# Decoder trunk on one core: where the second sums, a down half's last weights and the first seven-product chunk's weights are cast

## The chip, the cores and the metric

The kernel runs on one core of one Trainium2 chip. The metric is the device time of one launch in microseconds, as the median of several runs. One core has five engines with a queue each: PE (TensorE, matmuls; the profile shows its weight loads apart, as PEld), ACT (ScalarE), DVE (VectorE), POOL (GpSimd) and SP (SyncE, which here only issues loads of weights).

## What is computed

A decoder trunk of two layers on 512 tokens with 1024 features, all in float32. Each layer has a half-step SwiGLU network, a mixer, and a second half-step SwiGLU network; the first mixer is gated linear attention, the second a stick-breaking attention.

```python
D_MODEL = 1024
SEQ = 512
DEPTH = 2
D_FF = 2816

def swiglu(h, w_gate, w_up, w_down):
    return (jax.nn.silu(h @ w_gate) * (h @ w_up)) @ w_down

    for i in range(DEPTH):
        x = x + 0.5 * swiglu(rmsnorm(x, ffn1_norm[i]), ffn1_w_gate[i], ffn1_w_up[i], ffn1_w_down[i])
        h = rmsnorm(x, mix_norm[i])
        j = i // N_MIXERS
        if i % N_MIXERS == 0:
            y = gla_mixer(h, gla_w_in[j], gla_w_gk2[j], gla_b_gk[j], gla_o_norm[j], gla_w_out[j])
        else:
            y = sb_mixer(h, sb_w_in[j], sb_w_out[j])
        x = x + y.astype(x.dtype)
        x = x + 0.5 * swiglu(rmsnorm(x, ffn2_norm[i]), ffn2_w_gate[i], ffn2_w_up[i], ffn2_w_down[i])
    return rmsnorm(x, final_norm)
```

The change touches only the four SwiGLU networks, called FFN1 to FFN4 here (FFN1 and FFN2 lie around the first mixer, FFN3 and FFN4 around the second).

## The kernel before

**Split products.** Every float32 operand is cut into a high part, cast on ACT, and a low part, operand minus high part, made on DVE. A product is three matmuls: high times high, low times high, high times low. For weights the cast is L138 (names wh<-raw, wh<-rawd, wh<-s) and the low part L139 (wl); for activations both stand in `cut` (L838 and L839: nh/nl, th/tl, hh/hl).

**Stages.** FFN1 runs to about 337 us of the span, FFN2 from 545 to 870, FFN3 from there to 1206, FFN4 from 1414 to the end. Each has 11 chunks of 256 hidden columns, in groups (0,2), (2,4), (4,6), (6,8), (8,9), (9,11). For each chunk the gate product comes, then the up product. A group's down products follow later, between the chunks of the next groups.

**Seven products.** From chunk 2 on (`SEVEN`), gate and up are done as 2x2 blocks with seven products in place of eight (`seven`, L733 for the matmuls). Such a chunk has two entries in the list of work. `body_1` has three weights: a11 (128x512), the first sums s12 (128x1024) and a2 (128x1024). It makes product one into a PSUM bank w, has ACT copy w to z (L761, written ps_z<-ps_w), and goes on with product two into q, product three into w again and product four into z; L765 and L769 take q and w out in between. Product three may only write over w when the copy has read it. `body_2` has one weight, the second sums s34 (128x1024), for products five and six, and takes the other half of a2 for product seven. Sums are made on DVE (L718 and L719 for s12, L724 and L725 for s34).

The down products of groups 1 and 3 are done in the same way, in two halves each (`seven_down`, L394 for the matmuls). "First" to "fourth half" below are these in the order of an FFN. A half takes two loads of 128x1024, into two buffers named rawd. Its `body_1` has a11, the sums s12, and a2, which consists of two pieces of 128x512, one from each of the two loads; it makes two w products (for m of 0 and 1), copies both to z (L412), and has the products t1, t2 and b21, of which only b21 needs a2. Its `body_2` has the sums s34 for t3 and b22, ACT copies each w to a buffer u (L439, u<-ps_w) behind t3, and t4, with the other part of a2, writes over w. Results are added to x on DVE (L400).

**What sets the order.** `Feed.start` runs when an entry begins. It casts the weights of this entry and the two after it (`split`), as far as four buffers of 128x1024 suffice, makes the sums of one entry more, and issues the loads of six. Loads go out on SP, in order; a load waits until the last reader of its buffer is done. There are two buffers raw (1 MB) and two rawd (512 KB). A scheduler then puts the instructions of each engine into one order, from priorities, which `ahead` raises for what stands in it. `tc.issue_after(ins)` ties an instruction behind another. The chunks before `SEVEN` are plain blocks; `evac_u` (L886) makes the product of gate and up, and `close` cuts it to hh and hl for the down products, L80 ps_d.

The lines that the change starts from:

```python
            for e in self.q[i : i + 3]:
                used += sum(n * m >= 1024 for _, _, n, m in e.units)
                if used > 4:
                    break
                e.split()
            for e in self.q[i : i + 4]:
                e.view()
```

## Time and profile before

| what | value |
|---|---|
| median of 3 runs | 1778.77 us (1778.58 to 1780.93) |
| the profiled execution | 1778.36 us, span 1776.4 us |
| granted TensorE clock, mean | 0.999 |
| FFN1, FFN2, FFN3, FFN4 in the span | about 25 to 337, 545 to 870, 870 to 1206, 1414 to 1776 us |
| instructions | 31377 |

Rows of the profile are read thus: engine, line and operation, then what it writes and reads (`wl<-rawd,wh`), then shapes. In a timeline the first two numbers are start and duration in us; brackets tell how long the engine was idle before, and what released it. A row of the waits says who waited for whom, then total us, times, and the longest. Starts of neighbouring instructions on one engine lie closer together than their durations, since the next begins while the last drains; so a sequence is added up by starts.

### The profile page before, as it was taken

The page shows a single profiled execution, that of the slowest core. Times are in us where ns is not written, and L with a number is a line of the kernel's source. Part 1 is how long each engine was busy: PE and PEld are TensorE (multiplying, and loading weights), DVE is VectorE, ACT ScalarE, POOL GpSimd, SP SyncE. Part 2 cuts the span into 40 slices and gives each one's busy share as a digit, 9 for nine tenths or more (in the row PEclk, how much of TensorE's full clock was granted, in tenths as well). Part 3 has the DMA queues.
Part 4 walks back from the last instruction along what each step waited for, and adds up shares of the span by engine and source line. Part 5 has one row for each costly group of instructions (what it writes and reads, how often), then busy time and mean ns, then how long its engine had stood idle before and what let it go on. Part 6 is the DMA issues. An engine that isn't in the chain of part 4 may idle for free.

```text
span 1776.4 us, 31377 instructions
## 1 busy us (share of the span) xinstructions
PE 1755.4 (99%) x12714; PEld 1630.6 (92%) x12714; DVE 1509.6 (85%) x2474; ACT 1079.6 (61%) x1883; POOL 55.6 (3%) x77
## 2 busy tenths in 40 slices
PE   9999999999999999999999999999999999999998
PEld 8999999889888899999889999999888888999997
DVE  8999797786888989888798988967898679997986
ACT  7556556554655566555655555655888755565564
POOL 0000000200000000000000000010000000000000
PEclk9999999999999999999999999999999999999999
DMA  5543435422123433444434344342212234434441
GB/s 167 154 120 119 125 102 148 113 66 73 54 90 100 121 117 120 119 120 125 129 95 133 102 125 126 118 120 83 84 48 72 72 95 131 126 104 123 120 138 52
DMA packets 186388, 193.14 MB, mean 109 GB/s; under 512 B 4930, under 2 KB 171124, under 8 KB 186244
## 3 DMA queue, kind: packets, MB, share of 16 engines
q1 hardware_dynamic: 177760, 175.91, 31.7%
q0 software_dynamic: 8240, 14.95, 4.6%
q8 instruction: 99, 1.62, 0.4%
q14 instruction: 45, 0.37, 0.1%
q10 hardware_dynamic: 244, 0.29, 0.0%
HBM read 175.17 MB, written 2.10 MB: 100 GB/s over the span
## 4 chain that ended last, share of the span: by engine, by line
PE 60%; DVE 30%; ACT 5%; issue 3%; DMA 2%; SPq 0%; DVEq 0%; ACTq 0%
PE ps_w L733 13%; PE ps_d L80 12%; DVE wl L139 9%; PE ps_f L80 7%; PE ps_q L733 6%; PE ps_t L80 4%; PE ps_z L733 3%; PE ps_b L80 3%; PE ps_w L394 3%; ACT wh L138 2%; DVE x L400 2%; DVE hl L839 1%; PE ps_q L394 1%; DVE ts L848 1%; PE ps_z L1424 1%
## 5 line engine op out<-in xcount | busy, mean ns | idle before, releaser
L139 DVE TENSOR_TENSOR wl<-raw,wh 128x1024 fp32r<-128x1024 f32 x241 | 255.5, 1061 | 59.4 <-ACT wh L138 58.8
L138 ACT CAST wh<-raw 128x1024 fp32r<-128x1024 f32 x241 | 221.6, 920 | 77.8 <-PE ps_f L80 22.6
L139 DVE TENSOR_TENSOR wl<-s,wh 128x1024 fp32r<-128x1024 f32 x176 | 214.6, 1219 | 50.7 <-ACT wh L138 50.7
L733 PE MATMUL ps_w<-th,wh 128*128 128x256 f32 x864 | 239.4, 277 | 6.3 <-ACT ps_z L761 6.3
L733 PE MATMUL ps_w<-th,wl 128*128 128x256 f32 x864 | 237.6, 275 | 0.0
L733 PE MATMUL ps_w<-tl,wh 128*128 128x256 f32 x864 | 237.6, 275 | 0.0
L138 ACT CAST wh<-s 128x1024 fp32r<-128x1024 f32 x176 | 184.1, 1046 | 69.6 <-DVE s L719 19.4
L733 PEld LDWEIGHTS ps_w<-th,wh 128*128 128x128 f32 x864 | 165.8, 192 | 9.5 <-ACT ps_z L761 9.4
L80 PE MATMUL ps_f<-xh,wh 128*128 128x512 f32 x432 | 166.4, 386 | 0.0
L733 PEld LDWEIGHTS ps_w<-tl,wh 128*128 128x128 f32 x864 | 165.9, 192 | 0.0
L733 PEld LDWEIGHTS ps_w<-th,wl 128*128 128x128 f32 x864 | 165.8, 192 | 0.0
L80 PE MATMUL ps_f<-xh,wl 128*128 128x512 f32 x432 | 164.2, 380 | 0.5 <-DVE wl L139 0.5
L80 PE MATMUL ps_f<-xl,wh 128*128 128x512 f32 x432 | 163.9, 379 | 0.0
L80 PE MATMUL ps_d<-hl,wh 128*128 128x512 f32 x416 | 158.0, 380 | 1.7 <-DVE hl L839 1.7
L80 PE MATMUL ps_d<-hh,wh 128*128 128x512 f32 x416 | 158.0, 380 | 0.5 <-ACT hh L838 0.5
L80 PE MATMUL ps_d<-hh,wl 128*128 128x512 f32 x416 | 157.7, 379 | 0.0
L139 DVE TENSOR_TENSOR wl<-rawd,wh 128x1024 fp32r<-128x1024 f32 (+1 forms) x100 | 96.1, 964 | 15.8 <-ACT wh L138 15.1
L138 ACT CAST wh<-rawd 128x1024 fp32r<-128x1024 f32 (+1 forms) x100 | 82.9, 845 | 39.4 <-PE ps_d L80 25.6
L345 POOL DMA_DIRECT2D x<-d x53 | 45.8, 888 | 1510.1 <-ACT d L344 832.2
L80 PEld LDWEIGHTS ps_f<-xl,wh 128*128 128x128 f32 x432 | 81.6, 189 | 11.5
L80 PEld LDWEIGHTS ps_f<-xh,wl 128*128 128x128 f32 x432 | 81.7, 189 | 11.3 <-DVE wl L139 0.9
L80 PEld LDWEIGHTS ps_f<-xh,wh 128*128 128x128 f32 x432 | 81.7, 189 | 10.8
(355 smaller groups left out, 5331.4 us busy)
## 6 DMA issues: line engine op xcount, KB each, us to landing
raw<-in_ffn_w_gate_dram SPq DMA_DIRECT2D x43, 1024.0 KB, 5.4
raw<-in_ffn_w_up_dram SPq DMA_DIRECT2D x43, 1024.0 KB, 5.4
rawd<-in_ffn_w_down_dram SPq DMA_DIRECT2D x84, 512.0 KB, 3.8
x<-d POOLq DMA_DIRECT2D x53, 256.0 KB, 4.6
raw<-in_gla_w_in_dram SPq DMA_DIRECT2D x12, 1024.0 KB, 5.4
raw<-in_sb_w_in_dram SPq DMA_DIRECT2D x16, 512.0 KB, 3.7
raw<-in_gla_w_out_dram SPq DMA_DIRECT2D x4, 1024.0 KB, 5.1
raw<-in_sb_w_in_dram SPq DMA_DIRECT2D x4, 1024.0 KB, 5.2
```

The lines of the kernel that those rows point to most:

```text
L80: st["pe"] = nc.tensor.matmul(ps, l, r, start=first, stop=last).ins
L138: st["cut"] = nc.scalar.copy(h[:, k], part).ins
L139: nc.vector.tensor_tensor(out=l[:, k], in0=part, in1=h[:, k].bitcast(F32), op=ALU.subtract)
L345: nc.gpsimd.dma_start(xs[k], d, accum_op=ALU.add)
L394: st["pe"] = nc.tensor.matmul(ps, l_, r_, start=first and c + n == 0, stop=c == 1 and n == 2, skip_group_check=True).ins
L400: nc.vector.scalar_tensor_tensor(out=x, in0=ps, scalar=0.5, in1=x, op0=ALU.mult, op1=ALU.add)
L733: st["pe"] = nc.tensor.matmul(o, l_, r_, start=first and j + n == 0, stop=j == 3 and n == 2, skip_group_check=True).ins
L839: nc.vector.tensor_tensor(out=l, in0=t, in1=h.bitcast(F32), op=ALU.subtract)
L848: nc.vector.tensor_tensor(out=o, in0=p, in1=q, op=ALU.subtract)
L1424: nc.tensor.matmul(o_, l_, r_, start=first, stop=last, skip_group_check=True)
```

## The change

There are three parts.

1. The second sums s34 of a seven-product chunk are no longer cast as soon as the entry comes into reach. `Feed.start` stops at such an entry until its `body_1` has issued the copy z<-w (`copied`); `body_1` then has it split, with ACT's cast tied behind that copy.
2. In `seven_down` the third weight a2 is `held`: it isn't cast with the entry's other weights, but by `settle`, behind the second of the copies to z. Those copies are issued in `ahead`. `Feed.start` does not split beyond an entry that still holds a weight.
3. The two entries of the first seven-product chunk's gate are closed until the fourth hidden block of group 0 is cut to hh and hl; their sums and casts are then tied behind that cut (`st["closed"]`, `st["low"]`). The product in `evac_u` and the cut are issued in `ahead`.

No instruction of PE, POOL or SP changes its place. Lines shift: L138 becomes L165, L139 L166, L743 L786, L761 L804, L765 L809, L769 L813, L783 L827, L412 L445, L439 L473, L838 L884, L344 L376.

ACT in FFN1's first up chunk with seven products, around the copy z<-w. Names with s are sums, o are outputs of the gate and up products (L743 is the silu), raw is a weight as loaded. Before:

```order
L743 ACTIVATE o_736<-ps_z 128x256
L783 COPY u_835<-ps_w 128x256
L743 ACTIVATE o_737<-o_737 128x256
L138 COPY wh<-s_730 128x1024
L743 ACTIVATE o_736<-o_736 128x256
L743 ACTIVATE o_737<-ps_w 128x256
L138 COPY wh<-s_818 128x1024
L761 COPY ps_z<-ps_w 128x256
L138 COPY wh<-raw 128x512
L765 COPY o_875<-ps_q 128x256
L769 COPY o_874<-ps_w 128x256
```

Now:

```order
L786 ACTIVATE o_736<-ps_z 128x256
L827 COPY u_831<-ps_w 128x256
L786 ACTIVATE o_737<-o_737 128x256
L786 ACTIVATE o_736<-o_736 128x256
L786 ACTIVATE o_737<-ps_w 128x256
L804 COPY ps_z<-ps_w 128x256
L165 COPY wh<-s_730 128x1024
L165 COPY wh<-raw 128x512
L809 COPY o_871<-ps_q 128x256
L165 COPY wh<-s_814 128x1024
L813 COPY o_870<-ps_w 128x256
```

Both casts of sums, s_730 and s_818 (s_814 in the new numbers), stood ahead of the copy and stand behind it, and the second of them stands behind the copy from q too.

ACT in FFN1's second down half: the pair ps_z<-ps_w x2 is the copies of the two w products to z, the pair u the copies behind t3. Before:

```order
L743 ACTIVATE o_2005<-ps_w 128x256
L138 COPY wh<-rawd 128x1024
L412 COPY ps_z<-ps_w 128x256 x2
L138 COPY wh<-raw 128x512
L138 COPY wh<-s_2123 128x1024
L439 COPY u_2206<-ps_w 128x256 x2
L138 COPY wh<-raw 128x1024
L138 COPY wh<-s_2201 128x1024
```

Now:

```order
L786 ACTIVATE o_2000<-o_2000 128x256
L786 ACTIVATE o_2001<-ps_w 128x256
L445 COPY ps_z<-ps_w 128x256 x2
L165 COPY wh<-rawd 128x512 x2
L165 COPY wh<-raw 128x512
L165 COPY wh<-rawd 128x1024
L165 COPY wh<-s_2113 128x1024
L473 COPY u_2206<-ps_w 128x256 x2
L165 COPY wh<-raw 128x1024
L165 COPY wh<-s_2201 128x1024
```

The two casts of 128x512 from rawd, a2's two pieces, came earlier than these rows before (ahead of L783) and stand now behind the copies to z. The cast of 128x1024 from rawd, a later load, moved from ahead of those copies to behind a2's pieces, ahead of the u copies.

ACT in FFN1's fourth down half, where also two hh casts lie between. Before:

```order
L138 COPY wh<-rawd 128x512 x2
L783 COPY u_3414<-ps_w 128x256
L138 COPY wh<-s_3322 128x1024
L838 COPY hh<-o_3330 128x512
L138 COPY wh<-rawd 128x1024
L412 COPY ps_z<-ps_w 128x256
L838 COPY hh<-o_3331 128x512
L412 COPY ps_z<-ps_w 128x256
L138 COPY wh<-raw 128x512
L138 COPY wh<-s_3457 128x1024
L439 COPY u_3538<-ps_w 128x256 x2
L138 COPY wh<-raw 128x1024
```

Now:

```order
L827 COPY u_3408<-ps_w 128x256
L884 COPY hh<-o_3326 128x512
L445 COPY ps_z<-ps_w 128x256
L884 COPY hh<-o_3327 128x512
L445 COPY ps_z<-ps_w 128x256
L165 COPY wh<-rawd 128x512 x2
L165 COPY wh<-raw 128x512
L473 COPY u_3538<-ps_w 128x256
L165 COPY wh<-rawd 128x1024
L165 COPY wh<-s_3447 128x1024
L165 COPY wh<-raw 128x1024
L473 COPY u_3538<-ps_w 128x256
```

a2's two pieces moved from ahead of L783 to behind the second copy to z. Between the two u copies there are now three casts of 128x1024: of a rawd load, of sums and of a raw load.

The diff:

```diff
--- before.py
+++ after.py
@@ -112,32 +112,59 @@
 
         def __init__(self, units, body):
             self.units, self.body, self.W, self.views = units, body, None, None
+            self.second, self.v, self.held = False, None, None
+            self.open, self.behind = True, ()
 
         def view(self):
 
             if self.views is None:
-                self.views = [view(ch.load()) for ch, view, _, _ in self.units]
+                with self.queued():
+                    self.views = [view(ch.load()) for ch, view, _, _ in self.units]
             return self.views
 
-        def split(self):
+        def queued(self):
+            es = ExitStack()
+            for ins in self.behind:
+                es.enter_context(tc.issue_after(ins))
+            return es
+
+        def split(self, after=None):
             if self.W is None:
                 self.W = []
-                for r, (_, _, n, m) in zip(self.view(), self.units):
-                    few = n * m < 1024
-                    if few:
-
-                        h, l = (
-                            st["few"].tile([P, n * m], F32R, tag="v" + t, bufs=1, name="w" + t) for t in "hl"
-                        )
-                    else:
-                        h, l = (wp.tile([P, n * m], F32R, tag="w" + t, bufs=4, name="w" + t) for t in "hl")
-                    h, l = (t.rearrange("p (n m) -> p n m", m=m) for t in (h, l))
-                    pieces = r if isinstance(r, tuple) else (r,)
-                    for i, part in enumerate(pieces):
-                        k = slice(i * n // len(pieces), (i + 1) * n // len(pieces))
-                        st["cut"] = nc.scalar.copy(h[:, k], part).ins
-                        nc.vector.tensor_tensor(out=l[:, k], in0=part, in1=h[:, k].bitcast(F32), op=ALU.subtract)
-                    self.W.append((h, l))
+                for i, (r, (_, _, n, m)) in enumerate(zip(self.view(), self.units)):
+                    if i == self.held:
+                        self.W.append(None)
+                        continue
+                    with self.queued():
+                        self.W.append(self.parts(r, n, m, after))
+
+        @property
+        def waits(self):
+            return self.held is not None and (self.W is None or self.W[self.held] is None)
+
+        def settle(self, after):
+            i = self.held
+            _, _, n, m = self.units[i]
+            self.W[i] = self.parts(self.view()[i], n, m, after)
+            return self.W[i]
+
+        def parts(self, r, n, m, after):
+            few = n * m < 1024
+            if few:
+
+                h, l = (
+                    st["few"].tile([P, n * m], F32R, tag="v" + t, bufs=1, name="w" + t) for t in "hl"
+                )
+            else:
+                h, l = (wp.tile([P, n * m], F32R, tag="w" + t, bufs=4, name="w" + t) for t in "hl")
+            h, l = (t.rearrange("p (n m) -> p n m", m=m) for t in (h, l))
+            pieces = r if isinstance(r, tuple) else (r,)
+            for i, part in enumerate(pieces):
+                k = slice(i * n // len(pieces), (i + 1) * n // len(pieces))
+                with tc.issue_after(after) if after is not None else ExitStack():
+                    nc.scalar.copy(h[:, k], part)
+                nc.vector.tensor_tensor(out=l[:, k], in0=part, in1=h[:, k].bitcast(F32), op=ALU.subtract)
+            return h, l
 
     class Feed:
         def __init__(self):
@@ -147,13 +174,18 @@
             i = self.pos
             self.pos += 1
             used = 0
-            for e in self.q[i : i + 3]:
+            for n, e in enumerate(self.q[i : i + 3]):
+                if not e.open or e.v is not None and "copied" not in e.v and self.q[i + n - 2].second:
+                    break
                 used += sum(n * m >= 1024 for _, _, n, m in e.units)
                 if used > 4:
                     break
                 e.split()
+                if n and self.q[i + n - 1].waits:
+                    break
             for e in self.q[i : i + 4]:
-                e.view()
+                if e.open:
+                    e.view()
             for e in self.q[i : i + 6]:
                 for u in e.units:
                     u[0].load()
@@ -400,7 +432,7 @@
             nc.vector.scalar_tensor_tensor(out=x, in0=ps, scalar=0.5, in1=x, op0=ALU.mult, op1=ALU.add)
 
         def body_1(W):
-            a11, s, v["a2"] = W
+            a11, s = W[0:2]
             ws, zs, qs = [], [], []
             for m in range(2):
                 ws.append(psum("ps_w")[:, 0:H])
@@ -409,7 +441,9 @@
 
 
                 zs.append(psum("ps_z")[:, 0:H])
-                nc.scalar.copy(zs[m], ws[m])
+                with ahead():
+                    copied = nc.scalar.copy(zs[m], ws[m]).ins
+            v["a2"] = v["first"].settle(copied)
             yield
 
             ps = psum("ps_q")
@@ -451,7 +485,11 @@
 
         units = [(lower, lambda t: halves()[0], 2, 256), (lower, sums_12, 4, 256), (lower, lambda t: halves()[1::2], 4, 256)]
         feed.q.append(Entry(units, body_1))
+        feed.q[-1].held = 2
+        v["first"] = feed.q[-1]
         feed.q.append(Entry([(lower, sums_34, 4, 256)], body_2))
+        feed.q[-1].second = True
+        v["last"] = feed.q[-1]
 
     def back_tok(w, r0, nf, hs, done):
 
@@ -655,8 +693,13 @@
                         f_ = 0
                     if c >= self.SEVEN:
                         if f == 0:
+                            first_seven = c == self.SEVEN
                             self.sums_by = min(self.sums_by, len(feed.q) - base)
                             self.seven(g)
+                            if first_seven:
+                                self.opens = feed.q[-2:]
+                                for e in self.opens:
+                                    e.open = False
                     elif c not in self.SEVEN_UP:
                         feat(g, f_, self.evac_g, defer=d)
                     elif f == 0:
@@ -758,7 +801,8 @@
                 o0, o1 = v["o"] = [self.tp.tile([P, T], F32, tag="t", name=n) for n in ("o0", "o1")]
                 prod(w, a11, 0, half(0, 0))
                 with ahead():
-                    nc.scalar.copy(z, w)
+                    v["copied"] = nc.scalar.copy(z, w).ins
+                v["second"].split(v["copied"])
                 yield
                 prod(q, s, 0, lambda j: self.t_half(0, j))
                 with ahead():
@@ -819,6 +863,8 @@
             units = [(ch, lambda t: t[:, 0:4, 0:P], 4, P), (ch, sums_12, KD, P), (ch, lambda t: t[:, 4:8], 4, 256)]
             feed.q.append(Entry(units, body_1))
             feed.q.append(Entry([(ch, sums_34, KD, P)], body_2))
+            v["second"] = feed.q[-1]
+            feed.q[-1].second, feed.q[-1].v = True, v
 
         def t_half(self, i, j):
 
@@ -836,7 +882,7 @@
 
         def cut(self, h, l, t):
             st["closed"] = nc.scalar.copy(h, t).ins
-            nc.vector.tensor_tensor(out=l, in0=t, in1=h.bitcast(F32), op=ALU.subtract)
+            st["low"] = nc.vector.tensor_tensor(out=l, in0=t, in1=h.bitcast(F32), op=ALU.subtract).ins
             return h, l
 
         def normed_input(self):
@@ -883,15 +929,19 @@
             t = self.tp.tile([P, T], F32, tag="t", name="t")
             if not self.normed:
                 nc.vector.tensor_tensor(out=pair(t), in0=flat(ps), in1=pair(st["R"]), op=ALU.mult)
-            nc.vector.tensor_tensor(
-                out=pair(t), in0=flat(ps) if self.normed else pair(t), in1=pair(self.gates.pop(0)), op=ALU.mult
-            )
-            self.close(t, group)
+            with ahead():
+                nc.vector.tensor_tensor(
+                    out=pair(t), in0=flat(ps) if self.normed else pair(t), in1=pair(self.gates.pop(0)), op=ALU.mult
+                )
+                self.close(t, group)
 
         def close(self, t, group):
             h = self.hp.tile([P, T], F32R, tag="hh", name="hh")
             l = self.hp.tile([P, T], F32R, tag="hl", name="hl")
             self.hs[group].append(self.cut(h, l, t))
+            if group == 0 and len(self.hs[0]) == 4:
+                for e in self.opens:
+                    e.open, e.behind = True, (st["closed"], st["low"])
 
         def close_first(self, o0, group):
```

## The prediction

> **What bounds the kernel now.** I read the page first, then the chain, the waits, the windows, and last the timelines of ACT, DVE, SP and PE at the places that the change touches.
>
> ```profile
> span 1776.4 us, 31377 instructions
> PE 1755.4 (99%) x12714; PEld 1630.6 (92%) x12714; DVE 1509.6 (85%) x2474; ACT 1079.6 (61%) x1883; POOL 55.6 (3%) x77
> PE 60%; DVE 30%; ACT 5%; issue 3%; DMA 2%; SPq 0%; DVEq 0%; ACTq 0%
> 125.00:150.00 25.00, 24.84 (x223) 24.65 (x222) 24.86 (x44) 14.70 (x27) 0.00 (x0) 1.00 0.30 92
> ```
>
> TensorE is busy 99% of the span, at granted clock 1.00, so the change can win only the idle time in front of products, and loses whatever new idle time it makes. No matmul is added or taken away, and the orders on PE, POOL and SP are the same before and after; only ACT's and DVE's orders differ. The 30% that DVE holds in the chain, and the last row (a stretch of seven-product chunks: PE, PEld, DVE and ACT busy of 25.00 us, then clock and DMA), say that DVE has almost no slack there: an instruction that DVE must wait for is not caught up quickly. A change of over 0.2%, 3.6 us, can be told from none.
>
> The waits that the change aims at, as totals (us, times, longest):
>
> ```profile
> PEld ps_w L733 <- ACT ps_z L761: 9.4, 16, 1.3
> PEld ps_d L80 <- DVE hl L839: 2.8, 3, 1.2
> 154.52 0.38 PE L733 MATMUL ps_w<-th,wh 128*128 128x256 f32 x1 [0.46 <-ACT ps_z L761]
> 153.16 1.04 ACT L138 CAST wh<-s 128x1024 fp32r<-128x1024 f32 x1
> 154.09 0.38 ACT L761 COPY ps_z<-ps_w 128x256 f32<-128x256 f32 x1
> ```
>
> The fourth row is the cast of sums that sits in front of the copy z<-w (L761); the third product may only write over w when that copy is done, so PE waits until 154.52.
>
> **Part one: second sums cast behind the copy.** After the change ACT runs the copy first, and this cast and the one of sums before it come behind. The wait row says 9.4 us in 16 places. Each restart also stretches the first matmul, here 0.38 us where an undisturbed one has 0.28 (170.71, below): 0.1 us a time, 1.6 in 16 places, and a shorter wait or two below the table's notice. I take all of it off: **-11.2 us** (bounds -9.4 and -11.2). The casts that go behind the copy are needed only from the chunk's fifth product on, so their 0.93 us each (start to start, 153.16 to 154.09) are hidden by PE's products two to four.
>
> **Part two: a down half's last weights cast behind the copies L412.** This is the term that decides. In the second half of group 1 of FFN1:
>
> ```profile
> 165.81 1.15 ACT L138 CAST wh<-rawd 128x512 fp32r<-128x512 f32 x2
> 166.91 1.29 DVE L139 TENSOR_TENSOR wl<-rawd,wh 128x512 fp32r<-128x512 f32 x2
> 167.62 7.14 SPq L105 DMA_DIRECT2D rawd<-in_ffn_w_down_dram  x3
> rawd<-in_ffn_w_down_dram SPq DMA_DIRECT2D x3, 512.0 KB, 3.5
> 170.71 0.28 PE L394 MATMUL ps_w<-nh,wh 128*128 128x256 f32 x1
> 171.73 1.03 ACT L138 CAST wh<-rawd 128x1024 fp32r<-128x1024 f32 x1
> 172.67 0.64 ACT L412 COPY ps_z<-ps_w 128x256 f32<-128x256 f32 x2
> 174.93 1.05 ACT L138 CAST wh<-s 128x1024 fp32r<-128x1024 f32 x1 [1.07 <-PE ps_w L394]
> 177.04 0.38 ACT L439 COPY u<-ps_w 128x256 f32<-128x256 f32 x1 [1.06 <-PE ps_w L394]
> 178.80 0.28 PE L394 MATMUL ps_w<-nh,wh 128*128 128x256 f32 x1
> ```
>
> Before, the two 512 casts of a2 and their low parts are done by 168.2, before the half's first matmul (170.71). The low part is the last reader of its rawd buffer, and there are two such buffers: SP issues the next load the moment the first low part ends (167.62), so that its 3.5 us are over when ACT comes to the cast of that load (171.73).
>
> After, the same casts stand behind both L412 copies. Measured from 170.71: the second w product ends at about +1.5 (two products of 0.67 and a matmul's tail), the second copy at +1.8, the first cast 0.62 later at +2.4, its low part 0.68 later at +3.1. Only now does SP issue the load; it lands 3.5 us later at +6.6. ACT's order then has that load's cast, the 1024 cast of sums and, **behind** both, the copies of u (L439). Cast +6.6 to +7.55, sums to +8.5, first u copy to +8.9. The product t4 writes over the w bank that this copy reads, and PE reaches it at 178.80, which is +8.1: a stall of 0.8, with the reload 0.9 us. More rows bear on the size: the page's median load is 3.8 us, ACT already waits 4.0 us in eight places for loads of this kind, and in FFN4 the load takes longer:
>
> ```profile
> rawd<-in_ffn_w_down_dram SPq DMA_DIRECT2D x84, 512.0 KB, 3.8
> ACT wh L138 <- DMA rawd<-in_ffn_w_down_dram: 4.0, 8, 0.8
> rawd<-in_ffn_w_down_dram SPq DMA_DIRECT2D x3, 512.0 KB, 4.2
> 1601.38 1.05 ACT L138 CAST wh<-rawd 128x1024 fp32r<-128x1024 f32 x1 [0.76 <-DMA rawd<-in_ffn_w_down_dram]
> 1602.33 0.63 ACT L412 COPY ps_z<-ps_w 128x256 f32<-128x256 f32 x2
> ```
>
> With 3.5 us in FFN1, 4.2 in FFN4 and about the median in the two between, the stall is about 0.9, 1.2, 1.1 and 1.6: **+4.7 us** (bounds 3.4 and 7). The L412 pair at 1602.33 shows the mechanism at work today: its w products were long done, and it stood behind a cast that waited for a DMA. The Trainium skill ("Perfetto Trace Analysis", section "Tensor Engine Instruction (MATMUL, LD_WEIGHTS)") states that ACT and DVE take their instructions strictly first in, first out, and only PE may pull weight loads forward. The row at 1602.33 agrees; if ACT could pass a waiting cast, this and the next paragraph's terms would fall away and the sum would end below the time before.
>
> The fourth half is worse placed, since two hh casts stand between its copies:
>
> ```profile
> 277.11 0.28 PE L394 MATMUL ps_w<-nh,wh 128*128 128x256 f32 x1
> 278.29 1.05 ACT L138 CAST wh<-rawd 128x1024 fp32r<-128x1024 f32 x1 [0.40 <-DMA rawd<-in_ffn_w_down_dram]
> 279.54 0.61 ACT L838 CAST hh<-o 128x512 fp32r<-128x512 f32 x1
> 284.15 0.37 ACT L439 COPY u<-ps_w 128x256 f32<-128x256 f32 x1 [0.28 <-PE ps_w L394]
> 285.29 0.28 PE L394 MATMUL ps_w<-nh,wh 128*128 128x256 f32 x1
> ```
>
> From 277.11: second copy at about +2.0, first low part ended at +3.4 to +4 (DVE has hl of two o tiles to do as well), load landed at +7 to +7.8. ACT's order is then: u of m0 (in time), cast of the load, sums, a raw 1024 cast, and only then u of m1: three casts of 0.95 and a copy, +10.2 to +11. The second half of t4 is due at 285.29 + 0.67, or +8.85, and by the next part some 0.4 later. Stall 1.0 to 1.9, in FFN3 less, since there only two casts stand between: **+6.0 us** over four FFNs (bounds 3.6 and 9).
>
> **Part three: what DVE does in the halves.** The first and third halves have no load waiting in front of u, but a2's low parts now come between the half's first products and its adds to x:
>
> ```profile
> 132.46 0.28 PE L394 MATMUL ps_w<-nh,wh 128*128 128x256 f32 x1
> 134.59 1.22 DVE L139 TENSOR_TENSOR wl<-s,wh 128x1024 fp32r<-128x1024 f32 x1
> 136.33 0.75 DVE L400 SCALAR_TENSOR_TENSOR x<-ps_q,x 128x256 f32<-128x256 f32 x2
> 136.99 0.41 DVE L400 SCALAR_TENSOR_TENSOR x<-ps_w,x 128x256 f32<-128x256 f32 x1
> ```
>
> In time DVE gives up one low part of 1.14 us before the adds and gets two of 0.60, but these can't begin before ACT's casts behind the second copy. They end at about 137.1; the q adds (0.67) and the first w add (0.34) then end at 138.15, where t3, which writes the same bank, is due at 137.8 (132.46 and four products of 1.35, the pitch from 170.71 to 178.80 by six), 0.35 earlier; and product z waits some 0.2 for its low part. About 0.5 in eight halves and 0.45 in the four fourth halves: **+5.6 us** (bounds 0, if ACT reaches the casts 0.5 us sooner, and 9, at 0.75 each).
>
> **Part four: the first seven-product chunk.** In FFN2 (FFN4 alike) the last block of the plain chunks waits for its high and low parts, because low parts of the next chunk's weights stand in front:
>
> ```profile
> 602.72 1.21 DVE L139 TENSOR_TENSOR wl<-raw,wh 128x1024 fp32r<-128x1024 f32 x1
> 603.06 0.48 PE L80 MATMUL ps_d<-hh,wh 128*128 128x512 f32 x1 [0.23 <-ACT hh L838]
> 604.59 0.48 PE L80 MATMUL ps_d<-hl,wh 128*128 128x512 f32 x1 [0.83 <-DVE hl L839]
> 611.25 1.05 ACT L138 CAST wh<-s 128x1024 fp32r<-128x1024 f32 x1 [1.27 <-DVE s L719]
> 612.28 0.36 ACT L761 COPY ps_z<-ps_w 128x256 f32<-128x256 f32 x1
> 613.42 0.28 PE L733 MATMUL ps_w<-th,wh 128*128 128x256 f32 x1
> ```
>
> The two waits cost 0.40 and 1.00 us from matmul to matmul; after the change some 0.4 of the 1.4 stays. But the work put off, two low parts (2.3 us) and the sums, lands on DVE behind it. The sum for which ACT already waits 1.27 at 611.25 comes about 1 us later, its cast still stands ahead of copy z, and PE arrives 1 us earlier: the third product, due at 613.42 now, would wait 1.1 to 1.4. Net +0.2 in each of two; FFN3, which has no such wait to lose, gets some 0.8; FFN1 nothing. **+1.2 us** (bounds -2 and +3.5).
>
> **Sum.** -11.2 + 4.7 + 6.0 + 5.6 + 1.2 = **+6.3 us**. The profiled execution took 1778.36 us (span 1776.4), 0.4 below the median 1778.77; on the median's scale the forecast is 1785.
>
> **Rivals.** (a) *The gain is kept*, the other side: 1778.8 - 11.2 + 3 = 1770, about 1767 to 1775. It needs the late loads not to matter. For it speaks that the missing time is small, 0.8 us at second halves: a load landed 5.8 us after the half's start would do. Against it: the first low part ends at +3.1, and the load would have to take 2.7 us where the rows above have 3.5 to 4.2. Chance 0.15.
> (b) *An even trade*: the loads' stalls come (10.7) but DVE absorbs part three. -11.2 + 10.7 + 0 gives 1778, about 1775 to 1782. DVE's windows, full, speak against; that only half a microsecond a place is at stake speaks for. Chance 0.19.
> (c) *The delay spreads*: SP issues in order, so the raw loads of the next chunk, which stand behind the third rawd load, go out late too. Today the third is out by 174.76 (167.62 + 7.14) and the raw load only goes at 181.52:
>
> ```profile
> 181.52 0.37 SPq L105 DMA_DIRECT2D raw<-in_ffn_w_up_dram  x1
> ```
>
> After, the third waits for a low part at about +9 (179.7): hidden by under 2 us. Where the load takes over 4.2 us and DVE is 1 us late it shows, and the seven-product chunk behind then loses about 1 us in 6 to 8 places: 1792. Chance 0.09.
>
> **Chances and range.** My forecast has 0.57, its own range 1780 to 1793. All low bounds together give 1778.8 - 11.2 + 7 + 0 - 2 = 1773, all high ones 1778.8 - 9.4 + 16 + 9 + 3.5 = 1798, and neither is likely as a whole. 1771 to 1795 leaves out half of (a) and the far ends. Slower by over 0.2% (above 1782.3): most of my forecast, all of (c), 0.60. Within: 0.22, mostly (b) and the low end of mine. Faster (below 1775.2): (a) and the tail of (b), 0.18.
>
> **What would show it.** Right in part one: the PEld row for the copy z falls from 9.4 to under 3 us. Part two: a new row of L394's products waiting for the u copy, 8 times, 8 to 14 us, ACT's wait for the rawd load at casts up from 4.0 us to over 15, and rawd issues in the second half some 3 us behind its first matmul instead of 3 before. Part three: L394's products waiting for L400 or for the low part. Part four: the hl wait gone, and copy z left as a wait of 1 us once in FFN2, FFN3 and FFN4. The prediction is wrong if t4 finds its bank free in the second and fourth halves, or if low parts of a2 end under 2.3 us after the half begins.

## The result, and the profile after

The changed kernel takes 1794.2 us (median of 6 runs, 1792.57 to 1796.0) against 1779.91 us of the kernel before in the same comparison: ratio 1.0081, 95% interval 1.0068 to 1.0094. It is slower by 14 us; the forecast was 6 us slower. The time lies above the forecast's own range (1780 to 1793) and just inside the outer one (1771 to 1795).

The page of the changed kernel, first its span, then busy time by engine, then the engines' shares of the chain that ended last:

```profile
span 1791.2 us, 31323 instructions
PE 1758.6 (98%) x12714; PEld 1633.2 (91%) x12714; DVE 1506.4 (84%) x2474; ACT 1072.3 (60%) x1883; POOL 55.6 (3%) x77
PE 70%; DVE 16%; issue 6%; ACT 5%; DMA 3%; DVEq 0%; SPq 0%; ACTq 0%; POOLq 0%
```

The work is the same (12714 matmuls), and the busy times of ACT and DVE are within 8 us of before. What grew is time in front of matmuls. The waits of PE and its weight loads in the changed kernel (us in total, times, longest):

```profile
PE ps_w L426 <- ACT u L473: 11.8, 8, 1.9
PE ps_w L776 <- ACT ps_z L804: 4.0, 3, 1.5
PE ps_z L426 <- DVE wl L166: 1.5, 6, 0.3
PEld ps_w L426 <- ACT u L473: 13.3, 8, 2.1
PEld ps_w L776 <- ACT ps_z L804: 4.9, 4, 1.7
PEld ps_z L426 <- DVE wl L166: 2.7, 6, 0.5
PEld ps_w L426 <- DVE x L432: 1.9, 7, 0.3
PEld ps_d L80 <- DVE hl L885: 1.3, 2, 0.7
```

The 16 waits for the copy z<-w (L761 before, L804 now) are down to four. Against that stands a row that was not there before: the last product t4 of the second and fourth down halves waits for the u copies, eight times, as forecast. FFN1's second half in the timeline, ACT first, then DVE, SP and PE:

```profile
170.57 0.85 ACT L445 COPY ps_z<-ps_w 128x256 f32<-128x256 f32 x2
171.33 1.15 ACT L165 CAST wh<-rawd 128x512 fp32r<-128x512 f32 x2
172.37 0.62 ACT L165 CAST wh<-raw 128x512 fp32r<-128x512 f32 x1
176.38 1.05 ACT L165 CAST wh<-rawd 128x1024 fp32r<-128x1024 f32 x1 [3.39 <-DMA rawd<-in_ffn_w_down_dram]
177.34 1.04 ACT L165 CAST wh<-s 128x1024 fp32r<-128x1024 f32 x1
178.28 0.64 ACT L473 COPY u<-ps_w 128x256 f32<-128x256 f32 x2
171.99 1.30 DVE L166 TENSOR_TENSOR wl<-rawd,wh 128x512 fp32r<-128x512 f32 x2 [0.24 <-ACT wh L165]
172.71 0.97 SPq L105 DMA_DIRECT2D rawd<-in_ffn_w_down_dram  x2
178.70 0.38 PE L426 MATMUL ps_w<-nh,wh 128*128 128x256 f32 x1 [0.97 <-ACT u L473]
```

Read it as a chain: copies to z, a2's casts, their low parts, and only at 172.71 the load into the buffer thus freed. ACT stands 3.39 us with nothing to do but wait for that load. For the last 0.6 us of it a w bank is ready to be copied: where no cast stands in front (u_first below), the copy starts 6.3 us after the half's first matmul, and here the cast starts at 6.9. Then come cast, cast, copy, and t4 starts at 178.70. In FFN1's fourth half three casts stand between the two copies of u (283.96 and 287.50):

```profile
283.96 0.38 ACT L473 COPY u<-ps_w 128x256 f32<-128x256 f32 x1 [2.74 <-PE ps_w L426]
284.65 1.06 ACT L165 CAST wh<-rawd 128x1024 fp32r<-128x1024 f32 x1 [0.31 <-DMA rawd<-in_ffn_w_down_dram]
285.61 1.05 ACT L165 CAST wh<-s 128x1024 fp32r<-128x1024 f32 x1
286.56 1.04 ACT L165 CAST wh<-raw 128x1024 fp32r<-128x1024 f32 x1
287.50 0.36 ACT L473 COPY u<-ps_w 128x256 f32<-128x256 f32 x1
```

### The profile page after: what moved, and what is told of

Same layout as the page of the kernel before. It is cut to its first block, busy times and chain, and to the rows that moved or that the text cites. A ratio compares the mean times of both kernels' runs of the same rounds, so it can differ in the third digit from the quotient of the medians.

```text
span 1791.2 us, 31323 instructions
## 1 busy us (share of the span) xinstructions
PE 1758.6 (98%) x12714; PEld 1633.2 (91%) x12714; DVE 1506.4 (84%) x2474; ACT 1072.3 (60%) x1883; POOL 55.6 (3%) x77
## 4 chain that ended last, share of the span: by engine, by line
PE 70%; DVE 16%; issue 6%; ACT 5%; DMA 3%; DVEq 0%; SPq 0%; ACTq 0%; POOLq 0%
PE ps_w L776 19%; PE ps_d L80 12%; PE ps_q L776 9%; PE ps_f L80 8%; PE ps_z L776 5%; PE ps_t L80 4%; DVE wl L166 4%; PE ps_b L80 3%; PE ps_w L426 3%; ACT wh L165 2%; DMA rawd<-in_ffn_w_down_dram 2%; PE ps_z L1474 1%; PE ps_oT L1559 1%; PE ps_q L426 1%; PE ps_bt L80 1%
## 5 line engine op out<-in xcount | busy, mean ns | idle before, releaser
L166 DVE TENSOR_TENSOR wl<-raw,wh 128x1024 fp32r<-128x1024 f32 x241 | 255.5, 1061 | 50.4 <-ACT wh L165 49.8
L166 DVE TENSOR_TENSOR wl<-s,wh 128x1024 fp32r<-128x1024 f32 x176 | 214.5, 1221 | 76.2 <-ACT wh L165 75.6
L165 ACT CAST wh<-raw 128x1024 fp32r<-128x1024 f32 x241 | 221.8, 921 | 63.3 <-PE ps_f L80 22.6
L165 ACT CAST wh<-s 128x1024 fp32r<-128x1024 f32 x176 | 185.3, 1053 | 22.8 <-DVE s L762 11.2
L165 ACT CAST wh<-rawd 128x1024 fp32r<-128x1024 f32 (+1 forms) x100 | 82.7, 842 | 59.2 <-DMA rawd<-in_ffn_w_down_dram 28.9
L166 DVE TENSOR_TENSOR wl<-rawd,wh 128x1024 fp32r<-128x1024 f32 (+1 forms) x100 | 95.2, 966 | 21.8 <-ACT wh L165 21.7
L80 PEld LDWEIGHTS ps_f<-xh,wl 128*128 128x128 f32 x432 | 81.9, 189 | 11.2 <-DVE wl L166 0.9
```

The lines of the kernel that those rows point to most:

```text
L80: st["pe"] = nc.tensor.matmul(ps, l, r, start=first, stop=last).ins
L165: nc.scalar.copy(h[:, k], part)
L166: nc.vector.tensor_tensor(out=l[:, k], in0=part, in1=h[:, k].bitcast(F32), op=ALU.subtract)
```

## The experiments

PE's order is the same in all kernels here, so the traces can be compared stage by stage: the time between the starts of the same two matmuls. The first matmuls to 25 us of the span, which no edit touches, took up to 1.9 us more in some executions; the table leaves them out. Differences in us to the kernel before, from one profiled execution each ("to last" is from 25 us of the span to the last matmul). Some of these executions are not typical: those of mixed, no_part2 and next_sums were the fastest of their kernel, those of part2_only and u_first the slowest. Where a text below says what the products of one kind gain or lose, it is the same difference, added up over all of them.

| kernel | to last | median, us | ratio to the kernel before, 95% interval |
|---|---|---|---|
| the change | +13.6 | 1794.2 | 1.0081 (1.0068 to 1.0094) |
| no_part2 | +7.8 | 1788.55 | 1.0051 (1.0036 to 1.0066) |
| part1_only | +5.3 | 1784.31 | 1.0032 (1.0021 to 1.0043) |
| part2_only | +21.5 | 1798.81 | 1.0110 (1.0095 to 1.0125) |
| part3_only | +3.6 | 1782.1 | 1.0018 (1.0009 to 1.0027) |
| u_first | +2.4 | 1781.89 | 1.0016 (1.0007 to 1.0025) |
| u_ahead | +2.2 | 1782.46 | 1.0020 (1.0010 to 1.0029) |
| u_first_no3 | +3.2 | 1781.86 | 1.0014 (1.0005 to 1.0023) |
| next_sums | +0.6 | 1780.85 | 1.0009 (1.0 to 1.0017) |
| part1_ahead | -1.6 | 1777.24 | 0.9992 (0.9983 to 1.0001) |
| mixed | +0.8 | 1781.7 | 1.0012 (1.0003 to 1.0021) |
| mixed2 | -1.8 | 1777.38 | 0.9991 (0.9982 to 1.0) |
| part1_skip | -0.8 | 1777.09 | 0.9983 (0.9974 to 0.9992) |

**no_part2.** a2 is cast with the half's other weights again.

```diff
-        feed.q[-1].held = 2
+        feed.q[-1].held = None
...
-                with ahead():
+                with ExitStack():
                     copied = nc.scalar.copy(zs[m], ws[m]).ins
-            v["a2"] = v["first"].settle(copied)
+            v["a2"] = W[2]
```

> The changed kernel without its second part: a down half's a2 is cast with the half's other weights again, ahead of the copies to z. Theory (the trace after the change): the copies of u held behind late rawd loads cost 13.9 us, the late low parts of a2 another 6.6 us, and both come from the second part alone. The kernel should then take about 1794 - 20.5 = 1774 us, and the waits of L426 for u L473 and for wl L166 should be gone. Rival: DVE is so full that the first part's later casts of second sums make it late for everything behind; then a2's place hardly matters and the time stays above 1785 us.

1788.55 us. The theory was wrong by 14 us: the waits for u are gone, but other waits have come, and the time without the second part is still above that of the kernel before. The edit also takes the copies to z out of `ahead`, and the t2 products, which write over what these copies read, now lose 5.5 us to them (in the whole change they gain 0.9); t3 loses 4.3 us, in the whole change 3.3. The second part's terms do not stand beside the first's; the two share their cost.

**part1_only.** As no_part2, and besides the first chunk's entries are not closed, and `evac_u` stands as before.

```diff
-                            if first_seven:
+                            if False:
...
-            if group == 0 and len(self.hs[0]) == 4:
+            if False and len(self.hs[0]) == 4:
```

> The first part alone: second sums cast behind the copy z<-w, nothing else of the change. Theory: the copy's waits of 11.2 us go but for some 2 us of restarts and new short waits, 1780 - 9 = 1771 us. Rival (the later casts of second sums make DVE late): 1780 us or more, with new waits of L776 or L426 for low parts. The difference to the kernel without the second part is the third part's: theory +2.6 us, by the trace after the change.

1784.31 us: the rival. The first part does take the copy's waits away, but it loses more than it gains. The third products gain 9.8 us. The fifth products, the first to need the second sums, lose 4.6; in the down halves t2 loses 5.4 and t3 4.5. The waits of this kernel (first part alone):

```profile
PE ps_w L426 <- ACT ps_z L445: 3.7, 6, 1.1
PE ps_w L426 <- DVE x L432: 2.6, 6, 0.4
PE ps_w L776 <- DVE wl L166: 2.1, 4, 1.4
```

Of the three only the first is in the kernel before, with one wait of 0.3 us. The third is the fifth product waiting for the low part of the second sums; its longest wait is in FFN3, where that low part stands on DVE behind a sum that waits for a load:

```profile
1019.83 0.69 DVE L761 TENSOR_TENSOR s<-raw 128x512 f32<-128x512 f32 x1 [2.22 <-DMA raw<-in_ffn_w_gate_dram]
1020.43 1.22 DVE L166 TENSOR_TENSOR wl<-s,wh 128x1024 fp32r<-128x1024 f32 x1
```

The up chunk ahead of FFN1's first half and the half itself, ACT and then DVE and PE:

```profile
123.63 0.36 ACT L804 COPY ps_z<-ps_w 128x256 f32<-128x256 f32 x1
123.89 1.05 ACT L165 CAST wh<-s 128x1024 fp32r<-128x1024 f32 x1
122.74 0.69 DVE L762 TENSOR_TENSOR s<-s,raw 128x512 f32<-128x512 f32 x1
124.98 1.23 DVE L166 TENSOR_TENSOR wl<-s,wh 128x1024 fp32r<-128x1024 f32 x1 [1.55 <-ACT wh L165]
135.73 0.69 DVE L166 TENSOR_TENSOR wl<-raw,wh 128x512 fp32r<-128x512 f32 x1
136.33 0.76 DVE L432 SCALAR_TENSOR_TENSOR x<-ps_q,x 128x256 f32<-128x256 f32 x2
137.48 0.38 PE L426 MATMUL ps_w<-nh,wh 128*128 128x256 f32 x1 [0.43 <-DVE x L432]
```

DVE's next instruction is the low part of the sums whose cast was put off, and DVE waits 1.55 us for it. By the half DVE is only 0.4 us later than before, measured from the half's first matmul. Its order has changed as well: the low part of a raw weight (135.73) now stands ahead of the adds to x, where it stood behind three of them (137.32 in the kernel before). t3 at 137.48 waits for an add. No weight a2 is held in this kernel.

**part2_only.** Sums as before the change, no closed entries, a2 held.

```diff
-                if not e.open or e.v is not None and "copied" not in e.v and self.q[i + n - 2].second:
+                if not e.open:
...
-                v["second"].split(v["copied"])
+                v["second"].split()
```

> The second part alone: a2 of a down half cast behind the second copy to z, sums cast as before. Theory: 1780 + 20.5 = 1800 us, with L426 waiting for u L473 eight times, 12 to 14 us. Rival (it is the combination with later second sums that fills DVE): 1780 to 1787 us.

1798.81 us, as expected, though not for the expected sum. Its waits:

```profile
PE ps_w L426 <- ACT u L473: 10.3, 8, 2.2
PE ps_w L776 <- ACT ps_z L804: 7.4, 13, 1.8
```

The waits for u are there with no second sums put off; and PE still waits for the copies z<-w, up to 1.8 us where before the longest was 1.1. t3 waits for adds here too, in twelve halves (4.2 us with the restarts), though nothing of the first part is in this kernel; the kernel before has no such row:

```profile
PEld ps_w L426 <- DVE x L432: 3.5, 12, 0.3
```

First alone +5.3, second alone +21.5, third +3.6 would add up to 30; all three together have +13.6.

**u_first.** All of the change, and the weights of the entries behind a down half are cast behind its second copy of u.

```diff
-                e.split()
-                if n and self.q[i + n - 1].waits:
+                e.split(st.get("u"))
+                if n and self.q[i + n - 1].waits or e.half:
                     break
+            st["u"] = None
...
-                nc.scalar.copy(pair(u3[:, m]), flat(ws[m]))
+                st["u"] = nc.scalar.copy(pair(u3[:, m]), flat(ws[m])).ins
...
+        feed.q[-1].half = True
```

> All of the change, and besides the weights of the entries behind a down half are cast only behind its second copy of u, so that no cast waiting for a load stands ahead of a copy of u on ACT. Loads, their buffers and their issue stay. Theory (ACT runs in order, and the cast that waits for the load holds the copy): t4's waits for u, 13.9 us, go, the late low parts stay: 1780 to 1782 us. Rival (the late load itself is the bound, wherever its cast stands): the down product behind the half waits for its weights instead, and the time stays at 1790 us or above.

1781.89 us: the theory. Loads, buffers and the order on SP are those of the change; what differs is ACT's order and with it DVE's, and 12 of the 14 us are gone. t4 no longer waits at any place. So the late load costs what stands behind its cast on ACT, and little itself: the down products behind the halves wait 1.0 us for low parts of their weights, in two places, which they do not in the changed kernel.

**u_ahead.** All of the change, the u copies only raised in priority.

```diff
-                nc.scalar.copy(pair(u3[:, m]), flat(ws[m]))
+                with ahead():
+                    nc.scalar.copy(pair(u3[:, m]), flat(ws[m]))
```

> All of the change, and the copies of u only raised in priority: on ACT one cast of sums less (second halves), or two casts of 128x1024 fewer (fourth halves), stands between the load's cast and the copy; the load's own cast still stands in front. Theory (each cast in front costs its 0.95 us, the load's lateness the rest): the 13.9 us of waits for u fall by about 0.95 us in second halves and 1.2 to 1.9 in fourth, 8 to 10 us in all, to 1785 us. Rival (the load alone sets the wait): within 2 us of 1794.

```profile
PE ps_w L426 <- ACT u L474: 2.0, 2, 1.5
```

1782.46 us, 2.5 below the expected. The row has two of the eight waits left, and of the 13.9 us that t4 lost 3.2 are left (0.7 in FFN2's second half, 1.8 in FFN3's fourth, 0.3 or less elsewhere), although the load's cast still stands ahead of at least one copy. At most places the load alone was nearly in time, and the casts of sums and raw weights queued behind it made most of the wait.

**next_sums.** The kernel before, with casts tied behind the last copy z<-w that was issued before them.

```diff
-                        st["cut"] = nc.scalar.copy(h[:, k], part).ins
+                        with tc.issue_after(st["copied"]) if "copied" in st else ExitStack():
+                            nc.scalar.copy(h[:, k], part)
...
-                    nc.scalar.copy(z, w)
+                    st["copied"] = nc.scalar.copy(z, w).ins
```

> The kernel before, with one edit: casts that are issued behind a copy z<-w in the program are tied behind it on ACT. This moves one cast of 128x1024 (of the two that stood in front of a copy) behind the copy, and leaves the earlier one, with its low part on DVE, where it was. Theory (the first part's loss comes from the second sums' cast that DVE waits for: 1.55 us of idle DVE at 124.98 in the kernel with the first part alone, in a stretch where DVE was full): the copy's waits of 9 to 11 us go and nothing comes in their place, 1768 to 1772 us. Rival (DVE has no slack at all, so any cast put off is paid for in the down halves): 1778 us or more, with new waits of L394 for L400 and for copies to z.

1780.85 us: the rival. One cast moves instead of two, and the third products gain 5.9 us; but in the down halves t2 loses 3.7 us waiting for copies to z, and t3 3.0 waiting for adds. The waits of this kernel, and then the timeline of its ACT at FFN2's fourth half:

```profile
PE ps_w L734 <- ACT ps_z L762: 2.6, 5, 0.7
PE ps_w L395 <- ACT ps_z L413: 1.6, 2, 1.2
```

```profile
823.42 0.62 ACT L839 CAST hh<-o 128x512 fp32r<-128x512 f32 x1 [1.09 <-DVE o L747]
825.09 1.04 ACT L139 CAST wh<-rawd 128x1024 fp32r<-128x1024 f32 x1 [1.05 <-DMA rawd<-in_ffn_w_down_dram]
826.04 0.36 ACT L413 COPY ps_z<-ps_w 128x256 f32<-128x256 f32 x1
```

Here too ACT waits for DVE, then for a load, with a copy behind it.

**part1_ahead.** As part1_only, with the copies to z of the down halves in `ahead`.

```diff
-                with ExitStack():
+                with ahead():
                     copied = nc.scalar.copy(zs[m], ws[m]).ins
```

> The first part alone, and besides the copies to z of a down half (L445) are issued ahead, as the second part does it, with a2 cast early. Theory: the waits of L426 for these copies in the first part alone (3.7 us in the table of waits, some 5 us with the restarts) come from casts of sums that now stand in front of them; they go, and the time falls from 1784 to about 1779 us; L426's waits for L432 (2.6 us) stay. Rival (DVE's lateness is what counts): less than 1.5 us are gained.

1777.24 us, 7 us below part1_only, more than expected: the waits for L445 fall from 3.7 us to 1.0 (three times), and those for L432 from 2.6 to one of 0.2 us. By starts, t2 loses 2.1 us in place of 5.4, t3 1.3 in place of 4.5; the fifth products still lose 4.5. At FFN1's first half DVE has the same idle time as in part1_only and is as late, but its order is another:

```profile
125.17 1.22 DVE L166 TENSOR_TENSOR wl<-s,wh 128x1024 fp32r<-128x1024 f32 x1 [1.55 <-ACT wh L165]
135.93 0.75 DVE L432 SCALAR_TENSOR_TENSOR x<-ps_q,x 128x256 f32<-128x256 f32 x2
137.26 0.68 DVE L166 TENSOR_TENSOR wl<-raw,wh 128x512 fp32r<-128x512 f32 x1
```

The raw weight's low part is behind the adds again, and t3 is 0.15 us late in place of 0.7. So most of t3's wait in part1_only came from this order and not from DVE's idle time.

**part3_only.** The third part alone (the edits of no_part2 and both of part2_only).

> The third part alone. Theory (stage by stage in the traces of the changed kernel and of the two kernels without its second part): FFN3's first seven-product chunk loses some 1.6 us to a copy z<-w that stands behind a cast of sums, FFN2 and FFN4 trade 1.4 us of waits for hh and hl for about the same at the copy: 1780 to 1782 us, 1 to 2.6 above the kernel before. Rival (the third part gains where the first does not stand in its way): 1777 us.

1782.1 us, 3 us slower by the ratio, a little above the range. FFN2 gains 1.0 us where hl no longer waits so long, and loses 2.6 behind it, where the copies z<-w of the first two seven-product chunks come 1.4 and 0.9 us late; FFN4 likewise. FFN3 loses 1.65 us at the first copy and gets 1.3 back, since the next one no longer waits. In the changed kernel the wait in FFN3's first seven-product chunk looks like this, on ACT:

```profile
944.14 0.60 ACT L376 ACTIVATE d<-ps_d 128x512 f32<-128x512 f32 x1 [3.64 <-DMA x<-d]
944.63 1.04 ACT L165 CAST wh<-s 128x1024 fp32r<-128x1024 f32 x1
945.57 0.38 ACT L804 COPY ps_z<-ps_w 128x256 f32<-128x256 f32 x1
```

The copy comes 1.67 us late for the third product: an evacuation of d waited 3.64 us for an earlier transfer to leave its buffer, and the cast of sums and the copy stood behind it.

**u_first_no3.** u_first without the third part.

> First and second part with the weights behind a down half cast behind its u copies, without the third part. Theory (the third part costs 2.6 to 3.7 us wherever it stands): 1782 - 3 = 1779 us, level with the kernel before. Rival (the third part's cost hangs on the others): 1781 us or more.

1781.86 us, no different from u_first with it: the rival. The copies z<-w of the first seven-product chunks no longer come late, but the down products behind the halves now wait 3.1 us, in five places, for low parts of their weights. What the third part costs (3 us alone) hangs on the parts around it, and by these runs its share in the change can't be given.

**mixed and mixed2.** part1_ahead with a2 held only in each network's second half, whose u copies are in `ahead`; mixed2 besides casts the second sums of the chunk behind a down half early.

```diff
+        hold = part == 1 and r0 == 512
+        feed.q[-1].held = 2 if hold else None
...
-        feed.q[-1].second = True
+        feed.q[-1].second = False
```

> The first part, copies to z of the down halves ahead, and a2 held only in the second half of each network, there with its u copies raised ahead; no third part. Theory (the traces stage by stage: second halves lose 0.7 to 1.2 us where a2 is early and 0.05 to 0.2 where it is held and u raised): 2.5 to 3 us below the first part with copies ahead (1777.2), 1774 to 1775 us. Rival (the 0.2 us of those halves are only had when the halves before are later too): 1777 us.

> As the kernel before this one, and besides the second sums of the chunk right behind a down half are cast early, as before the change. Theory (there the copy never waited before, and the later cast makes the sixth product wait for its low part, 0.3, 0.3, 1.4 and 0.3 us): another 1.5 to 2 us, 1772 to 1773.5 us. Rival (the earlier cast takes the wait back to the copy z of that chunk): no change against the kernel before this one.

1781.7 and 1777.38 us. Both fell short: picking the better of two versions at each place from the stage table did not give the sum of the picks. A likely reason, not shown, is that each place starts with ACT and DVE as the place before left them. The last edit is worth 4 us by the medians and 2.6 in the two traces, more than the 2 expected.

**part1_skip.** part1_ahead with that last edit (`second = False` for down halves).

> The first part with the copies to z of the down halves ahead, a2 early, no third part, and the second sums of the chunk right behind a down half cast early, as before the change. Theory (the kernel without this last edit has waits for low parts of second sums in those chunks, about 2 us in all with FFN3's 1.3 us, and the edit takes them away): 1775 to 1776 us, some 3.5 below the kernel before. Rival (what one place gains, another gives back, as in the two kernels with a2 held in one half): 1777 us or more.

1777.09 us against 1779.83 in its own comparison: ratio 0.9983, interval 0.9974 to 0.9992, 3 us faster than the kernel before, a little short of the expected 3.5; the time itself is the rival's. The fifth products lose 1.4 us in place of 4.5, but t2 loses 6.0 in place of 2.1: what one place gains, another gives back. It is the only version clear of the kernel before; that it beats part1_ahead is not shown (intervals overlap, and its one trace is 0.8 us longer).

## Why the prediction was right in sign and short in size

The account of the changed kernel, by the starts of the delayed matmuls against the kernel before, in us:

| term | forecast | measured |
|---|---|---|
| part one, waits for copy z<-w | -11.2 | -8.5: third products -9.8, fifth products +1.3 |
| part two, waits for u | +4.7 and +6.0 | +6.3 and +7.6 (1.2 to 2.2 us in eight places) |
| part three, adds and low parts in the halves | +5.6 | +6.4: b21 waiting for a2's low part 3.1, t3 waiting for adds 3.3 |
| part four, first chunk | +1.2 | +2.5 (FFN3 1.7, not 0.8) |
| not forecast: t2 waiting for copies to z | 0 | -0.9 |
| sum | +6.3 | +13.4; the trace has +13.7 from the first to the last matmul, 0.3 of it in the first mixer |

The sign came out right since the four terms had the right places and signs; the size is off since all four came out on the costly side of their figures. (The forecast's own figures for part three, 0.5 in eight halves and 0.45 in four, add up to 5.8 and not 5.6, which changes nothing.)

**Part two** is the largest miss, 3.2 us, and was right in mechanism, place and count. The forecast had the first low part end 3.1 us after the second half's first matmul, and the load issued there; in the trace that matmul is at

```profile
169.52 0.28 PE L426 MATMUL ps_w<-nh,wh 128*128 128x256 f32 x1
```

and the issue at 172.71, 3.2 us behind. The size was short for two reasons. In the second halves ACT could begin the load's cast 3.7, 4.4, 3.9 and 4.1 us after the issue (FFN1 to FFN4), where I took 3.5 to 4.2. FFN2's is the longest:

```profile
721.31 0.97 SPq L105 DMA_DIRECT2D rawd<-in_ffn_w_down_dram  x2
725.72 1.05 ACT L165 CAST wh<-rawd 128x1024 fp32r<-128x1024 f32 x1 [4.12 <-DMA rawd<-in_ffn_w_down_dram]
```

In the fourth halves the loads took 3.3 to 3.9 us, but were issued 3.9 us behind the first matmul in FFN3 and FFN4 and 4.5 in FFN1 and FFN2, where I took 3.4 to 4.

```profile
ACT wh L165 <- DMA rawd<-in_ffn_w_down_dram: 28.9, 14, 4.1
```

This row is the tell-tale the forecast named: ACT's wait for these loads, 4.0 us before, now 28.9. u_first shows the mechanism by taking the stalls away with the loads left late.

**Part three** was right in mechanism too. On DVE a2's low parts stand between the half's first products and its adds, as forecast, and t3 waits (FFN1's first half, t3 at 137.14):

```profile
134.80 1.29 DVE L166 TENSOR_TENSOR wl<-rawd,wh 128x512 fp32r<-128x512 f32 x2
136.00 0.75 DVE L432 SCALAR_TENSOR_TENSOR x<-ps_q,x 128x256 f32<-128x256 f32 x2
137.14 0.38 PE L426 MATMUL ps_w<-nh,wh 128*128 128x256 f32 x1
```

part2_only has the late adds with nothing of the first part in it. part1_only has them too, with no a2 held, but there by a raw weight's low part that DVE takes ahead of the adds.

**The step that failed** is in part one: "the casts that go behind the copy ... are hidden by PE's products two to four". They are not hidden altogether, since their low parts come later too: the fifth products lose 1.3 us in the changed kernel and 4.6 with the first part alone. And the forecast put at nothing that the move changes ACT's and DVE's order in the down halves behind. Alone, the first part is worth not -11.2 us but +5 (1784.31 against 1779.12), and part1_ahead shows that most of the loss in the halves comes from this order: with the copies to z ahead, the same casts put off and, at FFN1's first half, the same idle time on DVE in front, it is level with the kernel before. In the changed kernel the second part brings these copies in `ahead` along, so the t2 waits of the first part alone don't appear in it; and t3 is late by 4.5 us with the first part alone, by 4.2 with the second alone, and by 3.3 with both. These are two reasons why the parts don't add up. Why the scheduler's order comes out so is not shown.

Two of the signs that the forecast named were missed: the PEld row for the copy z is at 4.9 us, not under 3, and the wait for hl at 1.3 us (2.8 before), not gone.

Rival (a), the gain kept, did not come; (b) had the loads' stalls but not the late adds. The time is close to the 1792 of (c), raw loads delayed on SP, but (c) did not happen: in FFN1 the raw load leaves at 181.32 us (181.52 before), and the chunks behind the second and fourth halves have no new wait. Of the 14.8 us of span, 1.1 lie behind the last matmul and are not accounted for. A third rawd buffer, which would free the load from the low part, was not tried.

## What to carry to other kernels

Before a cast is put behind something, look at who reads it next on the next engine (here DVE waited 1.55 us for it), and at the order that ACT and DVE then have in the stages behind: in part1_only one low part of 0.60 us ahead of the adds delayed t3 more than that idle time did. The last reader of a buffer also sets when the next load into it leaves; a cast put off by 6 us makes that load 6 us late (from 3.1 us ahead of the half to 3.2 behind its start), and whatever stands on the casting engine behind the load's cast is late too. Costs of such moves were not additive here, neither from part to part nor from place to place, so a version is measured whole.

## What the runs showed that I had not expected

Raising the priority of two small copies (u_ahead, part1_ahead) was worth 7 to 12 us, as much as the whole change set out to gain. And the same 512 KB load took 3.7 us at one place and 4.4 at another of the same kernel (second halves of FFN1 and FFN2: issued at 172.71 and 721.31, its cast begun at 176.38 and 725.72). At both a second load of the same size went out 0.6 us behind it, so that alone is not the reason; the cause is open.
